# A Strassen-like form with seven products for half of an MLP's down projections

## Chip, core and metric

The kernel runs on one core of one Trainium2 chip. The metric is the device time of one execution in microseconds (us). Before the change three runs took 2326.5, 2327.51 and 2328.44 us, median 2327.51 us.

## The reference

Two decoder layers over 256 tokens of width 2048 in float32: layer 0 with differential attention, layer 1 with a gated linear recurrence. After each of the two stands the same MLP, which this change concerns, and then a gated input embedding (`ple`).

```python
def rmsnorm(x, g):
    y = xf * lax.rsqrt(jnp.mean(xf * xf, axis=-1, keepdims=True) + EPS)
    return (y * g).astype(x.dtype)

def sqrelu_mlp(xn, w_up, w_down):          # w_up (2048, 8192), w_down (8192, 2048)
    return jnp.square(jax.nn.relu(xn @ w_up)) @ w_down

for i in range(2):
    h = h + mixer_i(rmsnorm(h, g_mix[i]))
    h = h + sqrelu_mlp(rmsnorm(h, g_mlp[i]), w_up[i], w_down[i])
    h = h + sigmoid(rmsnorm(h, g_ple[i]) @ w_ple_gate[i]) * (p[i] @ w_ple_proj[i])
```

## The kernel before

**Products in three parts.** Every float32 operand is split into two parts of type float32r, `hi` and `lo`, with `hi + lo` equal to the value. A product of 128 tokens, 128 k and 512 columns is then three matmuls into the same PSUM bank (`mm3`, lines 248 to 251): hi x hi, hi x lo, lo x hi. The weights come as fp32 from HBM and are split on the chip: ScalarE copies (line 255), VectorE subtracts (line 256).

**The weight stream.** `stream` (from line 332) walks over a list of groups. A group is one product over some k-tiles for 512 columns; its weights are cut into chunks of 4 k-tiles x 512 columns (1 MB, one DMA on SyncE's queue, `w_raw`, 3 buffers) and each chunk into two subs of 2 k-tiles (`w_hi` and `w_lo`, 4 buffers each: the slots). While sub j is multiplied, the loop issues loads two chunks ahead and splits three subs ahead (`W_SPLIT - 1`). The tile framework places all waits. It also orders each engine's instructions by a plan made at compile time, in which the order of the code is the priority, and gives a tile a free buffer of its pool.

**The MLP.** `mlp` (from line 628) works on 1024 of the 8192 hidden columns at a time. Two *up* groups give the hidden values transposed (`flip`: the weights stand in the array, the normed tokens, hi and lo side by side, move), each with 16 k-tiles x 4 blocks x 2 matmuls (line 391; 512 and 256 columns) into four banks. Its eviction (lines 644 to 646) adds the halves of each bank (ScalarE copy, VectorE add), does relu and square in one VectorE operation and splits the result into two tiles of the tag `big` (4 buffers of 8 KiB a partition). Four *down* groups follow, one for each 512 output columns, with 8 k-tiles: 2 token tiles x 8 k x 3 = 48 matmuls into two banks, after which line 589 adds each bank, scaled, to the residual `h`. The order is up(0), up(1), down(0), up(2), down(1) and so on, in units of 1024 columns, so down works on values evicted a stage ago. The last down groups feed the next norm: squares on ScalarE (line 302), transposes on TensorE through the two banks `tp` (line 317), scaled splits (lines 259 and 260).

PSUM has eight banks: six of the tag `acc` and two `tp`.

Of the kernel before, what the change touches and what calls it, by code (L numbers as in the profile page):

```python
# [17 lines left out]
P = 128  # L18
# [11 lines left out]
KC = 4  # L30
# [12 lines left out]
class Chunk:  # L43
    """Up to KC k-tiles of one weight column block, moved by one DMA."""

# [5 lines left out]
class Sub:  # L51
    """SK k-tiles of a chunk, split into two float32r parts."""

    own = None

# [4 lines left out]
class Group:  # L60
    """One product over nk k-tiles: [256 tokens, 512 columns], or its transpose where flip is set."""

    def __init__(self, w, k0, nk, n0, lhs, evict, flip=False):
        self.lhs, self.evict, self.nk, self.flip, self.subs, self.pre = lhs, evict, nk, flip, [], {}
        for c in range(0, nk, KC):
            n = min(KC, nk - c)
            r0 = (k0 + c) * P
            src = w[r0 : r0 + n * P, n0 : n0 + NB].rearrange("(c p) n -> p c n", p=P)
            ch = Chunk(src, n)
            self.subs += [Sub(ch, s) for s in range(0, n, SK)]  # L70


@with_exitstack
def trunk_kernel(ctx: ExitStack, tc, a, out):
# [35 lines left out]

# [1 line left out]
    state = {"tick": 0}  # L112
# [13 lines left out]

# [1 line left out]
    h = cp.tile([P, NT, D], F32, name="h")  # L128
# [117 lines left out]

# [1 line left out]
    def mm3(ps, lh, ll, rh, rl, start, stop):  # L248
# [34 lines left out]
    class Wide(Operand):  # L283
        """Both parts of a k-tile side by side: one [k, 512] moving operand."""

# [44 lines left out]

# [1 line left out]
    def stream(groups):  # L332
        subs = [s for g in groups for s in g.subs]
        chunks = []
        for s in subs:
            if not chunks or chunks[-1] is not s.chunk:
                chunks.append(s.chunk)
        cidx = {id(c): i for i, c in enumerate(chunks)}
        done = {"load": 0, "split": 0}

        def load_to(i):
            while done["load"] < min(i + 1, len(chunks)):
                c = chunks[done["load"]]
                c.raw = wraw.tile([P, KC, NB], F32, name="w_raw")
                if c.pre is not None:
# [6 lines left out]
                done["load"] += 1  # L352

        def split_to(i):
            while done["split"] < min(i + 1, len(subs)):
# [4 lines left out]
                else:  # L360
                    s.hi = wsp.tile([P, SK, NB], F32R, name="w_hi")
                    s.lo = wsp.tile([P, SK, NB], F32R, name="w_lo")
                    split(s.hi, s.lo, s.chunk.raw[:, s.k0 : s.k0 + SK])
                done["split"] += 1

        j = 0
        for g in groups:
            acc = [psum([P, NB]) for _ in range(4 if g.flip else NT)]
            kt = 0
            for i, s in enumerate(g.subs):  # L370
# [5 lines left out]
                if s.own is not None:  # L376
                    continue
                if g.flip:
                    x = g.lhs()
# [27 lines left out]

# [1 line left out]
    pT = {}  # L409
# [14 lines left out]

# [1 line left out]
    n0 = Norm(G_MIX)  # L426
# [197 lines left out]

# [1 line left out]
    FC = 1024  # L626
    NFC = DFF // FC
    FKT = FC // P

    def mlp(l, norm_in, norm_out):  # L630
        hid = {}

        def up_evict(c, half):
            """relu(.) ** 2 of a transposed product; the row factor squared goes onto the next product"""

            def evict(acc):
                if half == 0:
                    hid[c] = Operand(big([P, FKT, SEQ], F32R), big([P, FKT, SEQ], F32R))
                for b in range(2):
                    u = t2([P, 2, SEQ])  # L640
                    for i in range(2):
                        ps = acc[2 * b + i]
                        other = t1([P, SEQ])
                        nc.scalar.copy(other, ps[:, SEQ:])  # L644
                        nc.vector.tensor_tensor(u[:, i], ps[:, :SEQ], other, op=ALU.add)
                    nc.vector.scalar_tensor_tensor(u, in0=u, scalar=0.0, in1=u, op0=ALU.max, op1=ALU.mult)
                    ks = slice(half * 4 + 2 * b, half * 4 + 2 * b + 2)
                    split(hid[c].hi[:, ks], hid[c].lo[:, ks], u)

            return evict  # L650

        def up(c):
            for half in range(2):
                groups.append(
                    Group(a["w_up"][l], 0, KT_D, c * FC + half * NB, norm_in, up_evict(c, half), flip=True)
                )

        def down(c):
            for nb in range(4):
                groups.append(  # L660
                    Group(
                        a["w_down"][l], c * FKT, FKT, nb * NB, lambda kt, t, c=c: hid[c].lhs(kt, t),
                        residual_evict(nb, norm_out if c == NFC - 1 else None, lambda: norm_in().r2),
                    )
                )

        up(0)
        for c in range(1, NFC):
            up(c)
            down(c - 1)  # L670
        down(NFC - 1)

# [1 line left out]
    def ple(l, norm_in, norm_out):  # L674
# [49 lines left out]

# [1 line left out]
    w_in = a["w_in_rec"][0]  # L726
# [183 lines left out]

    # the first group takes x as it comes
    first = groups[0]
# [64 lines left out]
```

## Time and profile before

| | |
|---|---|
| median of three runs | 2327.51 us (2326.5 to 2328.44) |
| profiled execution, span | 2326.8 us |
| TensorE (PE) busy | 2308.8 us, 11467 matmuls |
| VectorE (DVE) busy | 1424.6 us |
| ScalarE (ACT) busy | 1193.6 us |
| DMA queue of the weights (q1) | 436.24 MB, 57.3% of 16 engines' span |

The page gives no time of the profiled execution other than its span, which lies among the runs. Times are microseconds unless marked ns. The busy time of PE is modelled and overlaps from one matmul to the next; how fast matmuls follow each other is seen in the start times.

### The profile page before, as it was taken

The numbers are of one execution on the slowest core, as the hardware profiler recorded it, in microseconds if no ns is written. First come the engines' busy times: TensorE is split into PE (matmuls) and PEld (weight loads), VectorE is DVE, ScalarE is ACT, GpSimd is POOL, SyncE is SP. The second block draws the span as 40 slices with busy tenths as digits, with TensorE's granted clock in tenths as the row PEclk, the third lists the DMA queues.
The fourth block names the chain that finished last, engine by engine and source line by source line (L and its number), as shares of the span: only waits on it lengthen the run. The fifth ranks groups of instructions, "written<-read, shape, count | busy, mean of one in ns | idle before, by whom it ended". The sixth has DMA issues, their size and how long they took to land.

```text
span 2326.8 us, 28564 instructions
## 1 busy us (share of the span) xinstructions
PE 2308.8 (99%) x11467; PEld 1946.9 (84%) x11467; DVE 1424.6 (61%) x1704; ACT 1193.6 (51%) x1594; POOL 44.7 (2%) x79
## 2 busy tenths in 40 slices
PE   8999999999999999999999999999999999999999
PEld 6888888888888888888888887888888888888887
DVE  6676655565565665566566767566565555565654
ACT  6555554444444444444558887454444444444453
POOL 2100000000000000000000000000000000000000
PEclk9999999999999999999999999999999999999999
DMA  7454555555565655655566565556565565555554
GB/s 241 163 185 163 165 179 181 185 195 189 191 197 184 198 188 192 196 185 181 189 193 219 187 212 181 181 182 198 184 197 190 191 197 184 198 189 191 177 199 148
DMA packets 225396, 438.95 MB, mean 189 GB/s; under 512 B 7582, under 2 KB 16416, under 8 KB 225264
## 3 DMA queue, kind: packets, MB, share of 16 engines
q1 hardware_dynamic: 224608, 436.24, 57.3%
q8 instruction: 89, 1.46, 0.3%
q0 software_dynamic: 608, 0.89, 0.2%
q14 instruction: 43, 0.35, 0.0%
q10 hardware_dynamic: 48, 0.02, 0.0%
HBM read 435.01 MB, written 2.10 MB: 188 GB/s over the span
## 4 chain that ended last, share of the span: by engine, by line
PE 94%; DVE 2%; ACT 2%; DMA 1%; issue 1%; SPq 0%; POOL 0%; DVEq 0%; ACTq 0%
PE acc L391 31%; PE acc L251 21%; PE acc L249 20%; PE acc L250 20%; PE tp L317 1%; DVE w_lo L256 1%; ACT w_hi L255 1%; DMA w_raw<-in_w_gate_x_dram 0%; DVE t L770 0%; DMA h<-in_x_dram 0%; PE tp L458 0%; DVE big L827 0%; ACT L810 0%; SPq L351 0%; ACT L788 0%
## 5 line engine op out<-in xcount | busy, mean ns | idle before, releaser
L256 DVE TENSOR_TENSOR w_lo<-w_raw,w_hi 128x1024 fp32r<-128x1024 f32 x808 | 987.4, 1224 | 781.4 <-ACT w_hi L255 779.9
L255 ACT CAST w_hi<-w_raw 128x1024 fp32r<-128x1024 f32 x808 | 849.0, 1052 | 979.8 <-PE acc L251 605.7
L391 PE MATMUL acc<-x,w_hi 128*128 128x512 f32 x2048 | 704.8, 394 | 0.0
L391 PE MATMUL acc<-x,w_lo 128*128 128x256 f32 x2048 | 547.8, 278 | 0.0
L249 PE MATMUL acc<-w_hi,x 128*128 128x512 f32 x1152 | 457.1, 397 | 0.0
L250 PE MATMUL acc<-w_lo,x 128*128 128x512 f32 x1152 | 450.2, 391 | 1.9 <-DVE w_lo L256 1.8
L251 PE MATMUL acc<-w_hi,x 128*128 128x512 f32 x1152 | 450.5, 391 | 0.0
L391 PEld LDWEIGHTS acc<-x,w_hi 128*128 128x128 f32 x2048 | 376.0, 188 | 78.6
L249 PE MATMUL acc<-w_hi,big 128*128 128x512 f32 x1024 | 399.7, 390 | 0.0
L251 PE MATMUL acc<-w_hi,big 128*128 128x512 f32 x1024 | 398.6, 389 | 0.0
L250 PE MATMUL acc<-w_lo,big 128*128 128x512 f32 x1024 | 398.4, 389 | 0.0
L391 PEld LDWEIGHTS acc<-x,w_lo 128*128 128x128 f32 x2048 | 384.7, 188 | 11.2
L251 PEld LDWEIGHTS acc<-w_hi,x 128*128 128x128 f32 x1152 | 216.8, 188 | 46.8 <-DVE x L256 0.2
L250 PEld LDWEIGHTS acc<-w_lo,x 128*128 128x128 f32 x1152 | 217.2, 189 | 45.0 <-DVE w_lo L256 3.0
L249 PEld LDWEIGHTS acc<-w_hi,x 128*128 128x128 f32 x1152 | 216.8, 188 | 41.7
L251 PEld LDWEIGHTS acc<-w_hi,big 128*128 128x128 f32 x1024 | 192.2, 188 | 40.3
L250 PEld LDWEIGHTS acc<-w_lo,big 128*128 128x128 f32 x1024 | 192.3, 188 | 39.8
L249 PEld LDWEIGHTS acc<-w_hi,big 128*128 128x128 f32 x1024 | 192.2, 188 | 39.0
L589 DVE SCALAR_TENSOR_TENSOR h<-acc,n_r,h 128x512 f32<-128x512 f32 x128 | 89.9, 744 | 0.0
L644 ACT COPY t<-acc 128x256 f32<-128x256 f32 x128 | 47.5, 371 | 22.8 <-PE acc L391 20.6
L259 ACT ACTIVATE x<-tp,cols_a 128x256 fp32r<-128x256 f32 (+1 forms) x72 | 35.7, 496 | 39.5 <-DVE x L260 39.5
L260 DVE SCALAR_TENSOR_TENSOR x<-tp,cols_a,x 128x256 fp32r<-128x256 f32 (+1 forms) x72 | 36.8, 511 | 18.8 <-ACT x L259 18.8
(173 smaller groups left out, 1064.2 us busy)
## 6 DMA issues: line engine op xcount, KB each, us to landing
w_raw<-in_w_up_dram SPq DMA_DIRECT2D x128, 1024.0 KB, 5.2
w_raw<-in_w_down_dram SPq DMA_DIRECT2D x128, 1024.0 KB, 5.1
w_raw<-in_w_qkv_dram SPq DMA_DIRECT2D x47, 1024.0 KB, 5.2
w_raw<-in_w_ple_gate_dram SPq DMA_DIRECT2D x32, 1024.0 KB, 5.2
w_raw<-in_w_in_rec_dram SPq DMA_DIRECT2D x32, 1024.0 KB, 5.5
w_raw<-in_w_o_attn_dram SPq DMA_DIRECT2D x16, 1024.0 KB, 5.2
w_raw<-in_w_o_rec_dram SPq DMA_DIRECT2D x16, 1024.0 KB, 5.1
w_raw<-in_w_ple_proj_dram SPq DMA_DIRECT2D x8, 512.0 KB, 3.7
```

Of the source, the lines that this page charges most:

```text
L249: nc.tensor.matmul(ps, lhsT=lh, rhs=rh, start=start, stop=False)
L250: nc.tensor.matmul(ps, lhsT=lh, rhs=rl, start=False, stop=False)
L251: nc.tensor.matmul(ps, lhsT=ll, rhs=rh, start=False, stop=stop)
L255: nc.scalar.copy(hi, src)
L256: nc.vector.tensor_tensor(lo, src, hi.bitcast(F32), op=ALU.subtract)
L259: nc.scalar.activation(hi, src, AF.Copy, scale=scale)
L260: nc.vector.scalar_tensor_tensor(lo, in0=src, scalar=scale, in1=hi.bitcast(F32), op0=ALU.mult, op1=ALU.subtract)
L317: nc.tensor.transpose(tp[:, i, t * P : (t + 1) * P], h[:, t, (k0 + i) * P : (k0 + i + 1) * P], ident)
L391: nc.tensor.matmul(o, lhsT=lh, rhs=rh, start=k == 0 and n == 0, stop=k == g.nk - 1 and n == 1)
L589: nc.vector.scalar_tensor_tensor(hb, in0=acc[t], scalar=scale()[:, t : t + 1], in1=hb, op0=ALU.mult, op1=ALU.add)
L644: nc.scalar.copy(other, ps[:, SEQ:])
```

## The change

The hidden columns are taken in 16 batches of 4 k-tiles (512 columns) a layer. Every second batch, with an even number, is multiplied in a *seven* form: for each pair of k-tiles the two token tiles and two k-tiles are a 2 x 2 matrix of blocks X, two k-tiles and two column blocks of 512 a matrix W, and the 2 x 2 product is formed from seven block products of sums of blocks in place of eight. The up eviction makes the sums S1 to S4 of X and splits them along with X; the sums of W (U1, T2, T3, T4) are made on VectorE from the raw chunks and split like weights. Seven partial sums P1 to P7 lie in seven PSUM banks and the plain batches' one left (Z) in the eighth, P3 and Z in the two `tp` banks.

A down group now covers 1024 output columns (one half) and mostly four batches: seven, plain, seven, plain. Its order: up(0), up(1), down(half 1; 0, 1), up(2), up(3), down(half 0; 0 to 3), up(4), up(5), down(half 1; 2 to 5), ..., up(14), up(15), down(half 0; 12 to 15), down(half 1; 14, 15). That is nine down groups a layer where there were 32. `middle` combines P1, P5, P6, P7 in SBUF after their last use, `evict` adds eight parts to `h`.

In the MLPs (`ring = 1`) raw chunks get a fourth buffer (of the tag `big`) and split weights two more slots (of `v4` and `big`), six in all. The relu and the square move from one VectorE operation to two of ScalarE. The rest of the diff drops comments and docstrings.

```diff
+S3, S1, S2, S4, X11, X12, X22, X21 = range(8)
+FORMS = (
+    ("W11", X11, "P1"), ("U1", S1, "P5"), ("T2", S2, "P6"), ("T3", S3, "P7"), ("W21", X12, "P2"),
+    ("T4", X22, "P4"), ("W22", S4, "P3"),
+)
+SUMS = {"U1": ("W11", "W12"), "T2": ("U1", "W22"), "T4": ("T2", "W21"), "T3": ("W12", "W22")}
+BT = 4
...
+class SevenGroup:
+    def products(self, i, s):
+        b, form, nj = self.what[i]
+        x, out = self.hid[b], []
+        if nj is None:
+            _, f, k = FORMS[form]
+            for j in range(2):
+                out.append((k,) + x.form(j, f) + (s.hi[:, j], s.lo[:, j]))
+        else:
+            n, j = nj
+            for t in range(NT):
+                for kk in range(SK):
+                    out.append((self.plain(n)[t],) + x.lhs(2 * j + kk, t) + (s.hi[:, kk], s.lo[:, kk]))
...
         def load_to(i):
-                c.raw = wraw.tile([P, KC, NB], F32, name="w_raw")
+                turn["raw"] += c.ring
+                if c.ring and turn["raw"] % (W_RAW + 1) == 0:
+                    c.raw = big([P, KC, NB])
+                else:
+                    c.raw = wraw.tile([P, KC, NB], F32, name="w_raw")
...
+        def split_form(s):
+            bl = s.blocks
+            src = bl.of(FORMS[s.form][0])
+            nc.scalar.copy(s.hi, src)
+            after = FORMS[s.form + 1][0] if s.form + 1 < len(FORMS) else None
+            if after in SUMS:
+                load_to(cidx[id(bl.chunks[1])])
+                one, two = (bl.of(nm) for nm in SUMS[after])
+                bl.sums[after] = t4([P, SK, NB])
+                nc.vector.tensor_tensor(bl.sums[after], one, two, op=ALU.add)
+            nc.vector.tensor_tensor(s.lo, src, s.hi.bitcast(F32), op=ALU.subtract)
...
         def split_to(i):
-                    s.hi = wsp.tile([P, SK, NB], F32R, name="w_hi")
-                    s.lo = wsp.tile([P, SK, NB], F32R, name="w_lo")
-                    split(s.hi, s.lo, s.chunk.raw[:, s.k0 : s.k0 + SK])
+                    turn["split"] += s.chunk.ring
+                    at = turn["split"] % (W_SPLIT + 2) if s.chunk.ring else 2
+                    if at == 0:
+                        s.hi, s.lo = (v4([P, SK, NB], F32R) for _ in range(2))
+                    elif at == 1:
+                        both = big([P, 2, SK, NB], F32R)
+                        s.hi, s.lo = both[:, 0], both[:, 1]
+                    else:
+                        s.hi = wsp.tile([P, SK, NB], F32R, name="w_hi")
+                        s.lo = wsp.tile([P, SK, NB], F32R, name="w_lo")
+                    if s.blocks is None:
+                        split(s.hi, s.lo, s.chunk.raw[:, s.k0 : s.k0 + SK])
+                    else:
+                        split_form(s)
...
+                if seven:
+                    prods = g.products(i, s)
+                    for q in prods:
+                        if q[0] not in acc:
+                            acc[q[0]] = ps_tp.tile([P, NB], F32, name="tp") if q[0] in ("P3", "Z") else psum([P, NB])
+                    for k, lh, ll, rh, rl, first, last in prods:
+                        nc.tensor.matmul(acc[k], lhsT=lh, rhs=rh, start=first, stop=False)
+                        nc.tensor.matmul(acc[k], lhsT=ll, rhs=rh, start=False, stop=False)
+                    for k, lh, ll, rh, rl, first, last in prods:
+                        nc.tensor.matmul(acc[k], lhsT=lh, rhs=rl, start=False, stop=last)
+                    if i == g.mid:
+                        g.middle(acc)
...
         def up_evict(b):
+                hid[b] = bt = batch(b)
+                for j in range(2):
+                    f = t4([P, 8, P]) if bt.seven else t2([P, 4, P])
...
+                        nc.vector.tensor_tensor(halves[i], two(ps[:, :SEQ]), two(other), op=ALU.add)
-                    nc.vector.scalar_tensor_tensor(u, in0=u, scalar=0.0, in1=u, op0=ALU.max, op1=ALU.mult)
+                    nc.scalar.activation(x, x, AF.Relu)
+                    nc.scalar.activation(x, x, AF.Square)
+                    if bt.seven:
+                        nc.vector.tensor_tensor(
+                            f[:, S3 : S1 + 1], f[:, X11 : X22 + 1 : X22 - X11],
+                            f[:, X21 : X21 + 1].broadcast_to([P, 2, P]), op=ALU.subtract,
+                        )
+                        nc.vector.tensor_tensor(f[:, S2], f[:, S1], f[:, X11], op=ALU.add)
+                        nc.vector.tensor_tensor(f[:, S4], f[:, X12], f[:, S2], op=ALU.subtract)
+                    split(bt.hi[:, j], bt.lo[:, j], f[:, :X21] if bt.seven else f)
...
+            def middle(acc):
+                c1, cb = t4([P, 2, NB]), t4([P, 2, NB])
+                keep["P1"], keep["M"], keep["B"], keep["N"] = c1[:, 0], c1[:, 1], cb[:, 0], cb[:, 1]
+                nc.scalar.copy(keep["P1"], acc["P1"])
+                nc.vector.tensor_tensor(keep["M"], keep["P1"], acc["P6"], op=ALU.subtract)
+                nc.vector.tensor_tensor(keep["B"], acc["P7"], keep["M"], op=ALU.add)
+                for k, o in (("M", "M"), ("N", "B")):
+                    nc.vector.scalar_tensor_tensor(
+                        keep[k], in0=acc["P5"], scalar=-1.0, in1=keep[o], op0=ALU.mult, op1=ALU.subtract
                     )
+            def evict(acc):
+                r2 = norm_in().r2
+                for t, n, ps, other in ((0, 0, "P2", "P1"), (1, 0, "P4", "B"), (0, 1, "P3", "M"), (1, 1, "Z", "N")):
+                    hb = h[:, t, hs[n]]
+                    for part in (acc[ps], keep[other]):
+                        nc.vector.scalar_tensor_tensor(
+                            hb, in0=part, scalar=r2[:, t : t + 1], in1=hb, op0=ALU.mult, op1=ALU.add
+                        )
+                if bs[-1] == NBT - 1:
+                    for n in range(2):
+                        norm_out().feed(2 * half + n)
...
+        for b in range(0, NBT, 2):
+            up(b)
+            up(b + 1)
+            down(int(b % 4 == 0), range(max(b - 2, 0), b + 2))
+        down(1, range(NBT - 2, NBT))
```

## Rows read from the trace of the kernel before

**Rows 1.** The page: span, busy time by engine, chain that ended last.

```profile
span 2326.8 us, 28564 instructions
...
PE 2308.8 (99%) x11467; PEld 1946.9 (84%) x11467; DVE 1424.6 (61%) x1704; ACT 1193.6 (51%) x1594; POOL 44.7 (2%) x79
...
PE 94%; DVE 2%; ACT 2%; DMA 1%; issue 1%; SPq 0%; POOL 0%; DVEq 0%; ACTq 0%
```

**Rows 2.** Costliest groups: line engine op, tiles, shapes, count | busy us, mean ns | idle before.

```profile
L255 ACT CAST w_hi<-w_raw 128x1024 fp32r<-128x1024 f32 x808 | 849.0, 1052 | 979.8 <-PE acc L251 605.7 <-PE acc L391 350.8 <-issue 11.6
...
L256 DVE TENSOR_TENSOR w_lo<-w_raw,w_hi 128x1024 fp32r<-128x1024 f32 x808 | 987.4, 1224 | 781.4 <-ACT w_hi L255 779.9
...
L391 PE MATMUL acc<-x,w_hi 128*128 128x512 f32 x2048 | 704.8, 394 | 0.0
...
L251 PE MATMUL acc<-w_hi,big 128*128 128x512 f32 x1024 | 398.6, 389 | 0.0
...
L589 DVE SCALAR_TENSOR_TENSOR h<-acc,n_r,h 128x512 f32<-128x512 f32 x128 | 89.9, 744 | 0.0
```

**Rows 3.** Chain in order of time: start us, length us, engine, tile, line.

```profile
537.50 44.40 PE acc L391 x256
...
845.89 0.23 PE acc L250
846.12 0.23 PE acc L251
```

**Rows 4.** Windows, layer 0: two up groups, four down groups, a whole period.

```profile
core 0: us, PE busy (x) PEld busy (x) DVE busy (x) ACT busy (x) POOL busy (x), PEclk, DMA share, GB/s
537.50:581.90 44.40, 44.40 (x258) 38.80 (x257) 24.63 (x28) 20.28 (x25) 0.00 (x0) 1.00 0.59 192
581.90:625.40 43.50, 43.50 (x193) 36.01 (x193) 27.14 (x30) 18.29 (x19) 0.00 (x0) 1.00 0.58 192
889.18:977.10 87.92, 87.92 (x450) 74.85 (x449) 51.79 (x57) 38.56 (x44) 0.00 (x0) 1.00 0.59 192
```

**Rows 5.** Groups by shape: smaller VectorE and ScalarE operations.

```profile
L644 ACT COPY t<-acc 128x256 f32<-128x256 f32 x128 | 47.5, 371 | 22.8 <-PE acc L391 20.6
...
L645 DVE TENSOR_TENSOR t<-acc,t 128x256 f32<-128x256 f32 x128 | 47.9, 416 | 0.0
...
L646 DVE SCALAR_TENSOR_TENSOR t<-t 128x512 f32<-128x512 f32 x64 | 43.6, 682 | 0.0
...
L256 DVE TENSOR_TENSOR big<-t,big 128x512 fp32r<-128x512 f32 x64 | 43.8, 684 | 0.0
...
L255 ACT CAST big<-t 128x512 fp32r<-128x512 f32 x64 | 39.7, 620 | 0.8
...
L302 ACT ACTIVATE t<-h 128x512 f32<-128x512 f32 x48 | 29.8, 623 | 0.0
...
L792 DVE TENSOR_TENSOR big<-t,t 128x256 f32<-128x256 f32 x16 | 6.8, 423 | 15.7 <-ACT t L790 15.7
...
L260 DVE SCALAR_TENSOR_TENSOR x<-tp,cols_a,x 128x256 fp32r<-128x256 f32 x64 | 30.8, 481 | 18.8 <-ACT x L259 18.8
```

**Rows 6.** Waits of SP's DMA queue (us, times, longest); down loads (KB, us to landing).

```profile
SPq L351 <- DVE w_lo L256: 1846.0, 364, 10.0
...
w_raw<-in_w_down_dram SPq DMA_DIRECT2D x128, 1024.0 KB, 5.1
```

**Rows 7.** ScalarE in order of time where up gives way to down.

```profile
845.97 1.05 ACT L255 CAST w_hi<-w_raw 128x1024 fp32r<-128x1024 f32 x1
846.91 0.62 ACT L255 CAST big<-t 128x512 fp32r<-128x512 f32 x1
```

**Rows 8.** Windows of the recurrence in layer 1 with VectorE or ScalarE busiest.

```profile
1300.00:1340.00 40.00, 37.78 (x186) 31.05 (x185) 36.10 (x51) 32.45 (x47) 0.00 (x0) 1.00 0.67 212
1390.00:1440.00 50.00, 48.43 (x232) 40.00 (x231) 37.69 (x47) 43.45 (x60) 0.00 (x0) 1.00 0.49 156
```

**Rows 9.** Groups: table loads.

```profile
L810 ACT ACT_TABLE_LOAD x11 | 14.1, 1283 | 0.2
```

More of the change, by code (lines that the diff above doesn't have):

```diff
@@ L43 @@
 class Chunk:
+    ring = 0
     def __init__(self, src, nk):
@@ L51 @@
 class Sub:
-    own = None
+    own, blocks, form = None, None, None
     def __init__(self, chunk, k0):
@@ new lines, with __init__, of, plain @@
+class Blocks:
+    def __init__(self, w, b, n0):
+        r0 = b * BT * P
+        rows = w[r0 : r0 + BT * P].rearrange("(c p) n -> p c n", p=P)
+        self.chunks = [Chunk(rows[:, :, n0 + i * NB : n0 + (i + 1) * NB], BT) for i in range(2)]
+        for c in self.chunks:
+            c.ring = 1
+        self.sums = {}
+    def of(self, name):
+        if name in self.sums:
+            return self.sums[name]
+        return self.chunks[int(name[2]) - 1].raw[:, int(name[1]) - 1 :: 2]
+class SevenGroup:
+    flip = False
+    def __init__(self, w, batches, n0, hid, middle, evict):
+        self.hid, self.middle, self.evict, self.subs, self.pre = hid, middle, evict, [], {}
+        self.what = []
+        for b, seven in batches:
+            bl = Blocks(w, b, n0)
+            if seven:
+                for i, (form, _, _) in enumerate(FORMS):
+                    s = Sub(bl.chunks[0 if form in ("W11", "W21") else 1], 0)
+                    s.blocks, s.form = bl, i
+                    self.subs.append(s)
+                    self.what.append((b, i, None))
+            else:
+                for n in range(2):
+                    for j in range(BT // SK):
+                        self.subs.append(Sub(bl.chunks[n], j * SK))
+                        self.what.append((b, None, (n, j)))
+        self.first, self.last = {}, {}
+        for i, (_, form, nj) in enumerate(self.what):
+            for k in [FORMS[form][2]] if nj is None else self.plain(nj[0]):
+                self.first.setdefault(k, i)
+                self.last[k] = i
+        self.mid = max(self.last[k] for k in ("P1", "P5", "P6", "P7"))
+    @staticmethod
+    def plain(n):
+        return (("P2", "P4"), ("P3", "Z"))[n]
+    def products(self, i, s):
[10 more added lines that the diff above has]
+                    out.append((self.plain(n)[t],) + x.lhs(2 * j + kk, t) + (s.hi[:, kk], s.lo[:, kk]))
+        res = []
+        for n, o in enumerate(out):
+            k = o[0]
+            same = [m for m, q in enumerate(out) if q[0] == k]
+            res.append(o + (self.first[k] == i and n == same[0], self.last[k] == i and n == same[-1]))
+        return res
@@ L335, in stream @@
         for s in subs:
-            if not chunks or chunks[-1] is not s.chunk:
+            if not any(c is s.chunk for c in chunks[-2:]):
                 chunks.append(s.chunk)
@@ L339, in stream @@
         done = {"load": 0, "split": 0}
+        turn = {"raw": 0, "split": 0}
         def load_to(i):
@@ L367, in stream @@
         for g in groups:
-            acc = [psum([P, NB]) for _ in range(4 if g.flip else NT)]
+            seven = isinstance(g, SevenGroup)
+            if seven:
+                acc = {}
+            else:
+                acc = [psum([P, NB]) for _ in range(4 if g.flip else NT)]
             kt = 0
@@ L623, in trunk_kernel, with is_seven, batch, up_evict @@
         groups.append(Group(a["w_o_attn"][0], 0, KT_D, nb * NB, lambda kt, t: oT().lhs(kt, t), residual_evict(nb, n_mlp0)))
-    FC = 1024
-    NFC = DFF // FC
-    FKT = FC // P
+    NBT = DFF // (BT * P)
+    SLOTS = 4
+    def is_seven(b):
+        return b % 2 == 0
     def mlp(l, norm_in, norm_out):
-        hid = {}
-        def up_evict(c, half):
-            def evict(acc):
[L637 to L640, printed above, removed]
+        hid, space = {}, {}
+        def batch(b):
+            if not is_seven(b):
+                both = big([P, 2, 2, 4, P], F32R)
+                return Batch(False, both[:, 0], both[:, 1])
+            if "x" not in space:
+                space["x"] = x32([P, 2, 2, 2, 7, P])
+            both = space["x"][:, b % SLOTS // 2]
+            return Batch(True, both[:, 0], both[:, 1])
+        def up_evict(b):
+            def evict(acc):
+                hid[b] = bt = batch(b)
+                for j in range(2):
+                    f = t4([P, 8, P]) if bt.seven else t2([P, 4, P])
+                    x = f[:, X11:] if bt.seven else f
+                    halves = (x[:, 0 : X21 - X11 + 1 : X21 - X11], x[:, X12 - X11 : X22 - X11 + 1])
@@ L641, in evict @@
                     for i in range(2):
-                        ps = acc[2 * b + i]
+                        ps = acc[2 * j + i]
                         other = t1([P, SEQ])
                         nc.scalar.copy(other, ps[:, SEQ:])
-                        nc.vector.tensor_tensor(u[:, i], ps[:, :SEQ], other, op=ALU.add)
-                    nc.vector.scalar_tensor_tensor(u, in0=u, scalar=0.0, in1=u, op0=ALU.max, op1=ALU.mult)
-                    ks = slice(half * 4 + 2 * b, half * 4 + 2 * b + 2)
@@ L667, in mlp @@
[L667 to L671, printed above, removed]
+                        two = lambda v: v.rearrange("p (t c) -> p t c", t=2)
+                        nc.vector.tensor_tensor(halves[i], two(ps[:, :SEQ]), two(other), op=ALU.add)
[8 more added lines that the diff above has]
+                        nc.vector.tensor_tensor(f[:, S4], f[:, X12], f[:, S2], op=ALU.subtract)
@@ new lines, in evict, with up, down @@
+                    split(bt.hi[:, j], bt.lo[:, j], f[:, :X21] if bt.seven else f)
+            return evict
+        def up(b):
+            g = Group(a["w_up"][l], 0, KT_D, b * NB, norm_in, up_evict(b), flip=True)
+            for s in g.subs:
+                s.chunk.ring = 1
+            groups.append(g)
+        def down(half, bs):
+            n0 = half * 2 * NB
+            hs = [slice(n0 + i * NB, n0 + (i + 1) * NB) for i in range(2)]
+            keep = {}
+            def middle(acc):
[7 more added lines that the diff above has]
+                        keep[k], in0=acc["P5"], scalar=-1.0, in1=keep[o], op0=ALU.mult, op1=ALU.subtract
+                    )
+            def evict(acc):
[7 more added lines that the diff above has]
+                if bs[-1] == NBT - 1:
+                    for n in range(2):
+                        norm_out().feed(2 * half + n)
+            groups.append(SevenGroup(a["w_down"][l], [(b, is_seven(b)) for b in bs], n0, hid, middle, evict))
```

25 lines of the change are left out of this document (11 added, 14 removed).

## The prediction

> **What bounds the kernel now.** First the page's busy shares: TensorE (PE) is busy 99% of 2326.8 us, VectorE (DVE) 61%, ScalarE (ACT) 51% [rows 1]. The chain that ended last says the same: 94% PE, two lines of DVE and ACT at 2% each [rows 1]. The span lies 0.7 us under the median of the three runs, 2327.51; I work with the span and add 0.7 at the end. Then the costliest groups: the down projections' 3072 products (three lines of 1024 with `big` as weights), the up projections' 2048 pairs, and 808 weight splits, 1.05 us on ACT and 1.22 us on DVE each [rows 2]. A matmul's own duration (389 ns) is not its pace, since they overlap; the chain in the third view gives the pace. A down product comes every 0.227 us, and two up groups stand as one unbroken piece of 44.40 us [rows 3]. The windows confirm it: 44.40 us of up and 43.5 us of down, PE busy for all of it, DVE for 24.6 and 27.1, DMA engines at 0.58 [rows 4]. One period of the MLP (two up groups, four down groups) is 87.92 us; 192 products in 43.52 us are 0.2267 us each. So the MLPs are bound by PE alone, with no stall to win back, and only fewer products can shorten them.
>
> What runs beside PE is paced by it: ACT's splits waited 350.8 and 605.7 us for PE to free a split buffer [rows 2], and the DVE behind them for ACT. The splits are thus limited by the four slots, not by DVE or ACT. That matters below.
>
> **The change part by part.**
>
> *Products removed.* A plain batch (4 k-tiles, two column blocks) takes 2 x 4 x 2 x 3 = 48 products; a batch in seven forms 7 x 2 x 3 = 42, of the same shape, 512 columns, with one weight load each as before. Each layer has 8 such batches, each for two column halves: 32 in all, 192 products fewer. At 0.2267 us [rows 3, 4] that is 43.5 us. Nothing suggests another pace for them. A period becomes 44.4 + 180 x 0.2267 = 85.2 us. Up projections and DMA bytes stay: each weight is still loaded once, 1 MB per chunk.
>
> *DVE added in down.* A plain batch needs 4 splits per half, a seven batch 7 and 4 sums. The trace has no sum of two weight blocks; it is a 128x1024 fp32 tensor_tensor like the split, so 1.22 us [rows 2], and not less than 0.94 (the pace of ACT's pass over as many elements, 845.97 to 846.91 [rows 7]) nor more than two of 0.68 [rows 5]. A seven batch then costs DVE 11 x 1.224 = 13.5 us against 42 x 0.2267 = 9.5 us of PE, a plain one 4.9 against 10.9. After form T3 of the group's last seven batch come the sums of products (`middle`): two of 0.68 and two of 0.74, 2.9 us; at the end of a group (`evict`) 4 x 0.74 + 4 x 0.68 = 5.7 us [rows 2, 5]. Before, the same h update took 8 x 0.74 per four groups.
>
> *Up eviction.* DVE loses the relu-square (0.68 each) and, for seven batches, gains a subtraction of 256 columns (0.42), two operations of 128 (0.29 by the step from 512 to 256) and a split of 896 in place of 512 (1.09, between 0.68 and 1.22). That makes 4 x 0.416 + 2 x 2.1 = 5.9 us for a seven batch and 3.0 for a plain one, 4.4 before. ACT gains relu and square, 0.62 each by its copies of that size [rows 5].
>
> *Sum by engine over one period* of two ups and a down group of four batches: DVE 16 x 1.224 (splits of up) + 8.9 (up evictions) + 8 x 1.224 + 22 x 1.224 (two plain, two seven batches) + 2.9 + 5.7 = 73.8 us of 85.2 (87%; 51.8 of 87.92 before [rows 4]); ACT 38 splits x 1.05, 8 copies x 0.37, 8 passes of relu and square x 0.62, 3.1 for the parts hi and 0.6 in `middle`, 51.7 us (61%). PE stays the longest. But in the down group alone DVE needs 45.3 us while PE needs 40.8. So it depends on work done ahead.
>
> *Work ahead.* Count from PE's end of the up groups. With six slots form n may be split when PE has left the sub six before it: forms 0 to 4 at -13.9, -11.1, -8.3, -5.6, -2.8 (up subs last 2.78 us). So 5 forms and their sums, up to 5 + 4 operations or 11 us of DVE, fit into the up group, where DVE is idle 45% [rows 4]. At 0 remain the up eviction and forms 5 and 6. The eviction is a chain over two engines: copy 0.37, add 0.42, relu, square, hi 0.62 each on ACT, lo 0.68, for two halves; I get its ACT part done at 4.3, so hi of form 5 at 5.3, lo at 6.6. PE wants that lo at 5 x 1.36 + 0.9 = 7.7. Cover left: 1.1 us. After that the plain batch (10.9 us of PE for 4.9 of DVE) lets DVE refill all slots, the second seven batch starts with up to 5 forms ready, `middle` has 15 us before its group ends, and the final `evict` (5.7 us) stands before up subs of 2.78 us with up to 5 ready. I cost all of this at 0 per period. A raw buffer: chunk pairs are held until form 6 is split, so the next pair lands about 13 us into the group (5.1 us each [rows 6]); it is needed by PE at 20.4. Also 0. SP's queue holds only these loads in the MLPs and waited for DVE's splits all along [rows 6].
>
> *Where cover is missing.* The last two groups of each layer follow each other without up groups between, and the first feeds the next norm. After its end DVE has 5.7 us of `evict`, then 8 scaled splits of 0.48, and forms 4 to 6 of the next batch (3.7 and a sum), all before PE has run 9.5 us; the transposes also need the two `tp` banks, which now hold P3 and Z. The work is about 14 us for 9.5, with some done before: a stall of 1.5 to 7, I take 4, twice. The feed after the last group now comes as one lump of 5.7 us before the gate's k-tiles 8 to 15 instead of 1.4 us before 12 to 15; PE has 13.6 us of other products meanwhile. I take 1, twice (0 to 4).
>
> Sum: 2326.8 - 43.5 + 8 + 2 = 2293.3, with 0.7 on top **2294**. The least is all of it hidden, 2284.
>
> **The rivals.**
>
> *A, the gain is lost (2334).* The engines' queues keep the order of the code, in which splits are only three subs ahead, and the up eviction stands in front of form 3. Then hi of form 3 comes at 5.3 where PE wants it at 4.1, and each of forms 4 to 6 keeps part of the delay: I add up 2.5 us for each of the 16 groups that follow an up eviction, 40 us on the forecast: 2334. For it: the lookahead count in the loop is unchanged at W_SPLIT - 1, and the eviction is longer by ACT's passes. Against it: in the trace a weight split at 845.97 went ahead of the eviction's own split at 846.91 though it is issued later [rows 7], so the order is not that of the code.
>
> *B, slower.* DVE becomes the bound in the down groups: 45.3 against 40.8 in 14 groups of four batches, 26.9 against 20.4 in 4 groups of two: 63 + 26 = 89 us of stall, 2373 if nothing is done ahead. The point of decision is 43.5 / 18 = 2.4 us of stall a group. For it: the recurrence's stretch with DVE at 90% lost 2.2 of 40 us of PE, and one with ACT at 87% 1.6 of 50 [rows 8]; 4% of the two MLPs' 1364 us would be 55, 2338. Against it: those stretches have PE waiting for chains through table loads and scans, while here weights depend on nothing but slots. I price it at 2350.
>
> *C, half of it.* The margin of 1.1 us at form 5 is missed by 1 to 2 us in each of these 16 groups, since every step of the chain is engine to engine: 2294 + 24 = 2318.
>
> *D, table loads.* A table load took 1.28 us [rows 9]. Were Relu in another table than the rest, 64 halves x 2 loads would put 164 us on ACT and some 5 us into each of the 16 tight places: about 2370. Square and Copy run side by side without a load [rows 5, 9]; Relu does not occur in this trace. The Trainium skill ("ScalarE: Activation LUTs", Table sets) says relu is in every set, which no row here shows.
>
> *E, the up evictions come onto the path.* ACT's passes over 512 columns took 0.62 us, and the DVE relu-square 0.68 in one pass [rows 5], so the move makes the chain 2 x 0.62 - 0.68 = 0.56 us longer per half. If PE waited for each of the 64 halves, that would be 36 us: 2330. Against it: no product needs a batch sooner than 9.5 us after its eviction. The Trainium skill ("ScalarE: Activation LUTs", Rules for kernel authors) tells to use VectorE, not ScalarE, for relu; the rows of this kernel bear it out as to the length of the pass, not as to what waits for it.
>
> **How the numbers follow.** Forecast 0.60 (own range 2283 to 2306), C 0.16, A 0.07, B 0.11, D 0.02, E 0.04. 0.2%, about 5 us, is what a measurement can tell from no change. The range runs from the least, 2284, less the 2 us by which the runs of before differ, to 2320, past C; beyond lie A, B, D, E and a little of C. Faster take the forecast, C and the lower ends of A and E: 0.78; within 0.2% the middle of A and E: 0.06; slower B, D and the upper ends of A and E: 0.16.
>
> **What would show it.** PE instructions fewer by 192 and a pace of 0.227 us inside a seven batch; a period of 85.2 us without PE waits, DVE near 87% in it; stalls only where two down groups meet (1 to 7 us) and at the gate's start. Wrong if PE waits for `w_lo` or `w_hi` in forms 3 to 6 of a group's first batch (A, C), in all seven batches (B), or if ACT shows table loads in the up eviction (D).

## The result, and the profile after

Four runs of the changed kernel took 2303.47 to 2304.05 us, median 2303.72; four of the kernel before beside them had a median of 2327.11. The ratio is 0.990, 95% interval 0.9885 to 0.9913: faster by 23 us. The forecast was 2294; the time lies within the range, 10 us above the forecast. The profiled execution took 2303.79 us with a span of 2301.9, so 1.9 us lie around the span where I had added 0.7.

The page of the changed kernel, to be held against [rows 1]: 192 products fewer, VectorE (DVE) busy 285 us longer, ScalarE (ACT) 162 us.

```profile
span 2301.9 us, 29004 instructions
...
PE 2277.8 (99%) x11275; PEld 1913.4 (83%) x11275; DVE 1709.6 (74%) x2048; ACT 1355.5 (59%) x1836; POOL 47.3 (2%) x79
```

PE is still "99% busy", yet the span shrank by 24.9 us and not by the 43.5 of the products. The windows show where to look: three periods, then each MLP from its first up product to the first product of the gate behind it. The second fence is one such window of the kernel before.

```profile
1827.21:1912.99 85.78, 85.78 (x437) 72.76 (x437) 68.13 (x77) 47.48 (x59) 0.00 (x0) 1.00 0.59 203
1912.99:1999.00 86.01, 86.01 (x437) 72.88 (x437) 69.24 (x77) 50.59 (x61) 0.00 (x0) 1.00 0.56 189
1739.58:1827.21 87.63, 86.30 (x438) 72.77 (x437) 69.56 (x77) 48.00 (x59) 0.00 (x0) 1.00 0.56 193
...
402.40:1098.40 696.00, 691.61 (x3513) 584.89 (x3513) 556.41 (x627) 396.48 (x495) 1.08 (x3) 1.00 0.56 191
...
1501.50:2197.40 695.90, 691.61 (x3514) 584.62 (x3513) 557.86 (x627) 395.68 (x496) 2.52 (x3) 1.00 0.55 190
```

```profile
403.70:1111.30 707.60, 707.60 (x3617) 602.26 (x3616) 421.31 (x466) 320.06 (x384) 1.08 (x3) 1.00 0.58 191
```

The period was 87.92 us [rows 4] and was to become 85.2. It repeats as 85.78, 86.01 and 87.63. In the first two PE is busy for every microsecond and still takes 0.6 and 0.8 too long: here products come slower. In the third it stands still for 1.3. The granted clock is 1.00 throughout, so the clock is not the reason.

The chain in order of time shows both. Under [rows 3] two up groups were one piece of 44.40 us; now, with the same 256 products, they are 44.70 to 44.99:

```profile
1769.81 14.67 PE acc L537 x83
1784.88 0.95 ACT w_hi L464
1785.83 1.04 ACT t L807 x2
1786.88 1.04 ACT t L808 x2
1788.32 0.62 ACT big L356
1788.94 0.96 ACT big L464
1789.94 0.51 PE acc L518
...
1827.21 44.70 PE acc L537 x256
...
1912.99 44.99 PE acc L537 x256
...
1999.00 44.90 PE acc L537 x256
...
2172.00 2.08 DVE h L848 x3
2174.10 0.68 ACT t L403 x2
2175.09 0.71 ACT t L403 x2
...
2176.16 0.94 ACT v L464
2177.14 0.50 PE acc L518
```

The top is the stall of the 87.63 period: the up groups end at 1784.48, ACT splits a form (L464), then runs the relu and the square of the up eviction (L807, L808) and the split of its result (L356, tag `big`), and only then the split of form 3 into the slot of tag `big`, for which PE waits. The bottom is the place where the last two down groups meet: `evict` on DVE, squares, then the split that PE waits for. Waits of PE in the down groups, total us, times, longest:

```profile
PE acc L518 <- ACT big L464: 5.3, 4, 1.3
...
PE acc L518 <- ACT w_hi L464: 1.3, 1, 1.3
PE acc L518 <- ACT v L464: 1.1, 1, 1.1
```

Four waits for `big` are two in each MLP. The slower pace shows in the start times of one form whose split weights lie in the slot of tag `v4` (shown as `v`): eight steps in 1.86 to 1.87 us, 0.233 us each, where a down product took 0.2267 on average by [rows 4].

```profile
1798.23 0.39 PE L518 MATMUL acc<-v,big 128*128 128x512 f32 x1
1798.46 0.39 PE L519 MATMUL acc<-v,big 128*128 128x512 f32 x1
...
1799.86 0.39 PE L519 MATMUL acc<-v,big 128*128 128x512 f32 x1
1800.09 0.63 PE L521 MATMUL acc<-v,big 128*128 128x512 f32 x2
```

To size the parts I charged each product of an MLP with the time from its start to the next start, and called a stall what goes beyond 0.2267 us in a step of over 0.44. A pair is the two products that the up groups take for one block and one k-tile:

| us in one MLP | before | after (layer 0, 1) |
|---|---|---|
| up, 1024 pairs | 355.75 | 359.07, 358.76 |
| down, 1536 or 1440 products | 349.03 | 329.51, 329.69 |
| stalls | 0.0 | 5.04, 5.14 |
| transposes of the next norm | 2.83 | 2.35, 2.28 |
| sum | 707.6 | 696.0, 695.9 |

In experiment 6, where the old pace is back, the 1440 products take 327.1. So in both MLPs together: 43.9 removed, 6.3 lost to the pace of up, 5.0 to the pace of down, 10.2 to stalls, 1.0 won back in the transposes and 1.5 outside the MLPs: 24.9, the difference of the spans.

### The profile page after: what moved, and what is told of

It reads as the page before. It is cut to its first block, busy times and chain, and to the rows that moved or that the text cites. A ratio compares the mean times of both kernels' runs of the same rounds, so it can differ in the third digit from the quotient of the medians.

```text
span 2301.9 us, 29004 instructions
## 1 busy us (share of the span) xinstructions
PE 2277.8 (99%) x11275; PEld 1913.4 (83%) x11275; DVE 1709.6 (74%) x2048; ACT 1355.5 (59%) x1836; POOL 47.3 (2%) x79
## 3 DMA queue, kind: packets, MB, share of 16 engines
q1 hardware_dynamic: 220256, 432.04, 55.5%
## 5 line engine op out<-in xcount | busy, mean ns | idle before, releaser
L357 DVE TENSOR_TENSOR w_lo<-w_raw,w_hi 128x1024 fp32r<-128x1024 f32 x465 | 564.2, 1221 | 304.5 <-ACT w_hi L356 304.4
L356 ACT CAST w_hi<-w_raw 128x1024 fp32r<-128x1024 f32 x465 | 486.6, 1051 | 419.4 <-PE acc L352 214.9
L537 PE MATMUL acc<-x,w_hi 128*128 128x512 f32 x1368 | 477.3, 396 | 0.0
L537 PE MATMUL acc<-x,w_lo 128*128 128x256 f32 x1368 | 368.5, 279 | 0.0
L537 PEld LDWEIGHTS acc<-x,w_hi 128*128 128x128 f32 x1368 | 251.9, 188 | 54.7
L537 PEld LDWEIGHTS acc<-x,w_lo 128*128 128x128 f32 x1368 | 257.8, 188 | 7.4
L464 ACT CAST w_hi<-t 128x1024 fp32r<-128x1024 f32 x85 | 89.2, 1051 | 128.8 <-PE acc L537 73.9
L537 PE MATMUL acc<-x,big 128*128 128x512 f32 (+1 forms) x688 | 127.7, 338 | 0.0
L356 ACT CAST w_hi<-big 128x1024 fp32r<-128x1024 f32 x87 | 90.7, 1050 | 62.6 <-PE acc L537 26.7
L537 PE MATMUL acc<-x,v 128*128 128x512 f32 (+1 forms) x672 | 124.8, 338 | 0.0
L537 PEld LDWEIGHTS acc<-x,big 128*128 128x128 f32 x688 | 107.9, 188 | 15.5
L537 PEld LDWEIGHTS acc<-x,v 128*128 128x128 f32 x672 | 105.9, 188 | 15.0
L471 DVE TENSOR_TENSOR w_lo<-w_raw,w_hi 128x1024 fp32r<-128x1024 f32 x64 | 78.0, 1219 | 31.9 <-ACT w_hi L464 31.9
```

Of the source, the lines that this page charges most:

```text
L357: nc.vector.tensor_tensor(lo, src, hi.bitcast(F32), op=ALU.subtract)
L464: nc.scalar.copy(s.hi, src)
L471: nc.vector.tensor_tensor(s.lo, src, s.hi.bitcast(F32), op=ALU.subtract)
L537: nc.tensor.matmul(o, lhsT=lh, rhs=rh, start=k == 0 and n == 0, stop=k == g.nk - 1 and n == 1)
```

## Experiments

Times are medians, with the ratio to the kernel before and its interval. "Up" is an MLP's up part as in the table.

**1. Is it the start of the `v4` tiles?** One of the two new split slots is the pair of `v4` tiles, which the attention used before as values. In the compiled program they begin at byte 218080 of a partition; the four old split slots, the tokens and `big` all begin 32 bytes past a multiple of 256 (61216, 93984, 162592). First the start was moved by 192 bytes:

```diff
+XW = SEQ + 8
...
-            xt = t4([P, 4, SEQ + 3])
+            xt = t4([P, 4, XW])
...
```

> The changed kernel with one size altered: the t4 buffers are 4224 instead of 4160 bytes, so that the v4 tiles, which serve as one of the six split slots, begin 32 bytes above a multiple of 128 like all other split slots (in the changed kernel: 96 above). Theory 1 (place): the products that read their weights from v4 are slow (233.3 ns against 226.7 ns) because of where the tile begins, and the slow spells of the up groups (2.83 us a sub in place of 2.77) start there. Then v4 products run at 226.7 ns, the up groups fall from 359 to about 356 us a layer, and the whole is 7 to 11 us faster than the changed kernel: about 2294. Theory 2 (activity): the pace falls because VectorE and ScalarE work more beside it and the slots only look different; then nothing changes, 2304. The three stalls of 1.5 us a layer stay in both.

Measured: 2301.69 (0.9888, 0.9874 to 0.9903), up 357.6 and 357.3; the products from `v4` now step by 229, 237 or 238 ns for the most part, in place of 233. So the place has an effect, but this was not a good place. Then all tiles were moved by 96 bytes as well, `v4` to 218368:

```diff
+    cp.tile([P, 24], F32, name="pad")
     ident = cp.tile([P, P], F32, name="ident")
```

> The same, and 96 bytes of padding ahead of all other tiles, so that every weight, operand and split tile begins at a multiple of 128 bytes instead of 32 above one. Theory 1 in its strong form: it is the distance to a 128-byte line that counts, and 32 above costs something as well, for all products: 512 columns would then take less than 226.7 ns, by up to 7 ns (the step between 226.7 and 233.3), and the whole would fall by up to 11000 x 6.6 ns = 70 us, to about 2230. In its weak form only unequal places of the two operands cost: then the result is that of the run before, about 2294. Theory 2: 2304.

2301.39 (0.9886, 0.9871 to 0.9901), up 357.5 and 357.1, and the down products of the other slots kept their 226.7. Both `v4` and the others now begin elsewhere, at the same distance from each other as in the run above, and up stays within 0.3 us: this speaks for the distance and against the start of each tile by itself.

**2. Is it the slot at all, without the change?** The kernel before with a fifth split slot of `v4` in its MLPs, and nothing else:

```diff
...
-                    s.hi = wsp.tile([P, SK, NB], F32R, name="w_hi")
-                    s.lo = wsp.tile([P, SK, NB], F32R, name="w_lo")
+                    turn["split"] += s.ring
+                    if s.ring and turn["split"] % (W_SPLIT + 1) == 0:
+                        s.hi, s.lo = (v4([P, SK, NB], F32R) for _ in range(2))
+                    else:
+                        s.hi = wsp.tile([P, SK, NB], F32R, name="w_hi")
+                        s.lo = wsp.tile([P, SK, NB], F32R, name="w_lo")
...
```

> The kernel before, with one part of the change alone: in the MLPs a fifth split slot made of the two v4 tiles, which begin 96 bytes above a multiple of 128. It has no work to win, since no product waited for a split. Theory 1 (place): a fifth of the down products, some 307 a layer, takes 233.3 instead of 226.7 ns (2 us a layer) and the up groups have slow spells (3 us a layer): 2327 + 10 = about 2337. Theory 2 (activity): VectorE and ScalarE do the same work as before, so no change: 2327.

2339.32 (1.0048, 1.0031 to 1.0065): 11 us slower, up 359.5 and 359.3, products from `v4` at 233 ns. Its chain has the long up pieces of the changed kernel:

```profile
1744.09 44.90 PE acc L397 x256
1832.81 44.98 PE acc L397 x256
1921.69 44.93 PE acc L397 x256
```

**3. Is the stall at form 3 one of order?** Splits five subs ahead in the MLPs, not three, so that form 3 is issued ahead of the up eviction:

```diff
-                split_to(j + W_SPLIT - 1)
+                split_to(j + (W_SPLIT + 1 if s.chunk.ring else W_SPLIT - 1))
```

> The changed kernel, but in the MLPs the loop issues splits five subs ahead instead of three, so that the first five forms of a down group stand ahead of the up eviction in the order of the code. Theory (buffers given out in the order of the code): form 3 of every third down group waits for its buffer of the tag big behind the plain batch's own buffer of that tag, which is taken by the eviction; with five ahead it no longer does, and the two stalls of 1.5 us in each MLP go: 2304 - 6 = about 2298. Rival (the eviction's ScalarE passes themselves hold form 3 back): the stalls stay, 2304. Second rival: early splits push the eviction back, PSUM banks come free later and PE stalls elsewhere: 2304 or more.

2295.58 (0.9862, 0.9847 to 0.9877), 8 us below the changed kernel. ScalarE in order of time: the split into `big` now comes 11 us ahead of relu and square, and no such wait is left. Stalls are 1.5 and 1.3 us an MLP; up stays at 359.1 and 358.8. So the order of issue explains the stalls at form 3, and with them 1.4 us at the meeting of the last two groups, and not the pace.

```profile
1770.47 1.05 ACT L464 CAST big<-t 128x1024 fp32r<-128x1024 f32 x1
...
1781.90 1.15 ACT L807 ACTIVATE t<-t 128x512 f32<-128x512 f32 x2
```

**4. Fewer slots.** Five, without `v4`, splits four ahead; and four, without `v4` and `big`, three ahead:

```diff
-                    at = turn["split"] % (W_SPLIT + 2) if s.chunk.ring else 2
-                    if at == 0:
-                        s.hi, s.lo = (v4([P, SK, NB], F32R) for _ in range(2))
-                    elif at == 1:
+                    at = turn["split"] % (W_SPLIT + 1) if s.chunk.ring else 2
+                    if at == 1:
...
-                split_to(j + W_SPLIT - 1)
+                split_to(j + (W_SPLIT if s.chunk.ring else W_SPLIT - 1))
```

> The changed kernel without the split slot of the two v4 tiles (five slots: four and the one of the tag big), with splits issued four subs ahead. Theory (the v4 slot sets the pace): without it no product runs at 233.3 ns, the up groups stay in the fast pace (about 356 us a layer in place of 359) and down products at 227.2 ns on average: 4.5 us a layer, 9 us in all, better than the run with five subs ahead (2295.6): about 2287, if five slots are enough; stalls at forms 3 to 6 of a down group would show that they are not, 1 to 3 us for each of 16 groups, up to 2320. Rival (the pace has to do with the seven form or with busier VectorE and ScalarE): up groups stay at 359 us a layer and the time at 2296 or above.

```diff
-                    at = turn["split"] % (W_SPLIT + 2) if s.chunk.ring else 2
+                    at = 2
```

> The changed kernel with four split slots as before the change (the fourth raw buffer stays). Theory of the prediction (work ahead makes the seven form free): with three forms ready at the start of a down group, forms 3 to 6 come behind the up eviction and cost about 2.5 us in each of 16 groups, and the place where two down groups meet loses more: 2304 + 40 + 5, less 9 for the pace that the extra slots cost: about 2340. Rival: the lookahead is worth nothing, since the loop issues only three subs ahead anyway: 2304 - 9 = 2295.

Five slots: 2291.22 (0.9843, 0.9829 to 0.9858), up 355.75 in both layers, stalls of 2.9 and 5.5 us where the last two groups meet. Four slots: 2295.47 (0.9861, 0.9845 to 0.9878), up 355.75, small waits that lengthen its down products by 3 us an MLP (330.3) and 1.8 us of stalls. I had expected 2340 of four slots; the rival's 2295 came out, though not its reason, that lookahead is worth nothing: the small waits show that it covered some of the work. The change was 8 us faster without its two new slots than with them: as placed and as ordered, they cost more in pace and in stalls at form 3 than they bring in cover.

**5. The eviction's passes.** Relu and square in one VectorE operation again (one run):

```diff
-                    nc.scalar.activation(x, x, AF.Relu)
-                    nc.scalar.activation(x, x, AF.Square)
+                    nc.vector.scalar_tensor_tensor(x, in0=x, scalar=0.0, in1=x, op0=ALU.max, op1=ALU.mult)
```

> The changed kernel with relu and square in one VectorE operation as before, in place of two on ScalarE. Theory (rival E is wrong, up evictions lie beside PE): only the two stalls of 1.5 us a layer shorten, since form 3's split gets ScalarE about 2 us sooner: 2298 to 2304. If E were right in part, 10 us or more would go: 2294 or less. If VectorE's load were what counts (0.68 us more for each of 64 halves): slower than 2304.

2297.12, 6.6 us below the changed kernel; PE no longer waits for `big`, and up is 359.1 and 358.8. With ACT's two passes gone form 3 comes in time: the same stall, mended from its other end.

**6. Place first.** As 3, and the `v4` tiles get their place ahead of others (byte 159520), by a small write at the start:

```diff
+    for _ in range(2):
+        nc.gpsimd.memset(v4([P, 8]), 0.0)
     rows_g = t1([P, P])
...
```

> The run with five subs ahead and six slots (2295.6), with only the place of the tags in memory altered: the v4 tiles come first in their pool (byte 159520 of a partition in place of 218080), all other tags of the pool move up by 8192 bytes. If the pace of the v4 products comes from where these tiles lie in memory, it changes: up groups 356 to 359 us a layer, v4 products other than 233.3 ns, and at best 2287. If it comes from the slot being two tiles of a tag that others use too, and not from its place, nothing changes: 2296.

2285.74 (0.9819, 0.9804 to 0.9834): 18 us below the changed kernel. Up is 355.75 in both layers, products from `v4` come every 226.7 ns (eight in 1.81 us in the second fence), and its up pieces are 44.40 us long and 85.20 apart:

```profile
1644.53 44.40 PE acc L539 x256
1729.73 44.40 PE acc L539 x256
1814.93 44.40 PE acc L539 x256
```

```profile
1786.21 0.39 PE L520 MATMUL acc<-v,big 128*128 128x512 f32 x1
...
1788.02 0.84 PE L523 MATMUL acc<-v,big 128*128 128x512 f32 x3
```

**7. Which rule of place?** In 6 the tiles are lower in memory and also a multiple of 256 bytes from the other operands. Two paddings in front of `v4` in the version of 3 keep them behind all other tiles and change only the distance (64 bytes: 208 floats become 16):

```diff
...
+            if hp == 0:
+                nc.gpsimd.memset(wk.tile([P, 208], F32, tag="pad", name="pad", bufs=1), 0.0)
```

> ahead5 with 832 bytes a partition of padding in front of the two v4 tiles, which now begin at byte 218912 of a partition, still behind all other tiles. Theory of distance: the pace depends on the distance from the v4 tile to the other operand tiles (tokens hi at 93984, split slots from 61216) modulo 1024; it was 192 in ahead5 and 0 in v4_first, and is 0 here. Then the v4 products come every 226.7 ns, the up groups of an MLP take 355.8 us and the run about 2286. Rival, place: what is far up in memory is slow; then up 359 and 2296, as ahead5.

> ahead5 with 64 bytes a partition of padding in front of the v4 tiles (byte 218144): their distance to the other operand tiles is 256 modulo 1024. Distance modulo 1024 or 512: slow products of about 233 ns, up 358 to 359 us, 2294 to 2297. Distance modulo 256 or less: 226.7 ns, up 355.8, 2286. Place (far up is slow): 2296.

832 bytes: 2285.70 (0.9818, 0.9803 to 0.9833). 64 bytes: 2285.24 (0.9816, 0.9802 to 0.9831). Both have up at 355.75 and 226.7 ns from `v4`. So 64 bytes of padding are worth 10 us beside experiment 3. Height in memory is refuted, and so is a modulus of 512 or 1024. Up pieces of the 64-byte version:

```profile
1729.28 44.40 PE acc L537 x256
1814.48 44.40 PE acc L537 x256
```

| start of `v4` | distance to the other operands, modulo 256 | step of its products, ns | up, us |
|---|---|---|---|
| 218080 (after, 2, 3, 5) | 192 | 233 | 358.8 to 359.5 |
| 218272, 218368 (1) | 128 | 224 to 238, mixed | 357.1 to 357.6 |
| 159520, 218144, 218912 (6, 7) | 0 | 226.7 | 355.75 |

**8. The slot in the kernel before, well placed.** 2 with the edit of 6:

> The kernel before with a fifth split slot of v4 tiles, as before_v4 (2339), but v4 tiles given their place first, 0 modulo 1024 from the other operand tiles. Distance or place: the slot costs nothing and gains nothing, 2326 to 2328, products 226.7 ns in both up and down. Rival, a fifth slot is itself harmful (other tags, other semaphores): about 2339 again.

2327.20 (0.9998, 0.9989 to 1.0008), up 355.75. What 2 lost was place alone; a fifth slot by itself neither costs nor gains there.

**9. The eviction again, with both causes gone.** 6 with the edit of 5:

> v4_first with relu and square in one VectorE operation again. relu_dve took away the 3 us of stall an MLP at form 3, but v4_first has none left there. If the eviction only mattered for the big slot: the same as v4_first, 2285 to 2287. If the two ScalarE passes still hold something up (the stalls of 1.3 to 1.5 us an MLP where two down groups meet are on VectorE's side, so more VectorE work could also lengthen them): 2282 or 2289.

2285.73 (0.9819, 0.9804 to 0.9834), the same as 6. Once form 3 is split ahead, it made no difference here which engine does relu and square.

## Why the prediction was right, and where it missed

**Products removed: right.** 192 products went, and at the pace of [rows 3, 4] they are worth the 43.5 us of the sum. In the version of experiment 6 the period is 85.20 us, the predicted figure. The bytes did not quite stay: the queue of the weights moved 432.04 MB, not 436.24, since the new list of chunks loads the recurrence's gate weights (`w_gate_a`, `w_gate_x`) 8 times each and not 16. That lies outside the MLPs, where all differences together are 1.5 us.

**"Nothing suggests another pace" was the step that failed**, and with it "up projections stay": +11.3 us against 0. I had taken the pace of a product as given by its shape. It also depends on the place of the slot. The diff showed that two slots of other tags come in; the trace before could not show their pace, as its MLPs never multiply from `v4`, and I gave the step no upper bound. But that trace did show that the shape alone does not give the pace: the second up group of each MLP took 22.59 us, the third and those behind it 22.20, PE busy throughout and the granted clock 1.00. Layer 0, second and third group of the kernel before, columns as in [rows 4]:

```profile
426.83:449.42 22.59, 22.59 (x129) 19.60 (x128) 13.50 (x18) 10.81 (x14) 0.00 (x0) 1.00 0.59 190
449.42:471.62 22.20, 22.20 (x130) 19.41 (x128) 13.43 (x18) 10.82 (x14) 0.00 (x0) 1.00 0.58 186
```

This slow group stands unchanged in experiments 4 and 6 to 9, so a badly placed slot is not the only thing that brings the slower pace.

**The range held by its width.** It had been drawn past C, whose waits did not come, and a pace that the prediction had not considered took that room. The 9.7 us above the forecast are the 11.3 of pace and 1.2 around the span, less smaller terms.

**Stalls: the sum right by luck, the places wrong.** 10 us were predicted (8 at the meeting of the last two groups, 2 at the gate) and 10.2 measured, but 4.2 at the meeting, none at the gate and 6.0 at form 3, which I had at 0. There rival A's mechanism holds in part. In the code form 3 takes its `big` buffer after the batch that the eviction writes, and its split is issued after it; forms 4 and 5, issued later still but into `w_hi`, were split before it (1781.74 and 1784.77 in the fence below, form 3 at 1788.84). That the shared tag is what holds the order is my reading of this; the run of experiment 3 shows that an earlier issue removes the wait. From [rows 7] I had concluded that the order is not that of the code; that row shows a split into `w_hi`, whose slots are not shared with the eviction. A period issues 38 subs, two more than a multiple of six, so only every third period has the `big` slot at form 3: 4 stalls of 1.5 us, not 16 of 2.5.

**Work ahead, margin at form 5: wider than predicted.** The up groups ended at 1784.48. Form 5's hi part was expected 5.3 us later, behind the eviction; even in a stalled period it began at 1784.77, ahead of relu and square, and form 6's at 1789.79. PE did not wait for forms 4 to 6 (C wrong). ScalarE from form 4 on:

```profile
1781.74 1.05 ACT L464 CAST w_hi<-w_raw 128x1024 fp32r<-128x1024 f32 x1 [4.89 <-PE acc L537]
...
1784.77 1.06 ACT L464 CAST w_hi<-t 128x1024 fp32r<-128x1024 f32 x1
1785.72 1.15 ACT L807 ACTIVATE t<-t 128x512 f32<-128x512 f32 x2
1786.78 1.14 ACT L808 ACTIVATE t<-t 128x512 f32<-128x512 f32 x2
1787.82 1.12 ACT L356 CAST big<-t 128x512 fp32r<-128x512 f32 x2
1788.84 1.04 ACT L464 CAST big<-t 128x1024 fp32r<-128x1024 f32 x1
1789.79 1.05 ACT L464 CAST w_hi<-w_raw 128x1024 fp32r<-128x1024 f32 x1
```

**B wrong; DVE's load over-estimated.** 73.8 us a period were predicted, 68.1 to 69.6 measured (79 to 81%). The durations were right: the sum of weights takes 1.22, as assumed, the split of 896 columns 1.08. In the three period windows of the changed kernel the durations add up to 73.1 to 74.1. But operations on one engine overlap a little, so their sum is more than the busy time; [rows 7] had shown it on ScalarE, where a pass of 1.05 was followed 0.94 after its start. Two sums in a row on VectorE in experiment 6 start 1.13 us apart:

```profile
2158.01 1.22 DVE L472 TENSOR_TENSOR t<-t,w_raw 128x1024 f32<-128x1024 f32 x1
2159.14 1.22 DVE L472 TENSOR_TENSOR t<-w_raw 128x1024 f32<-128x1024 f32 x1
```

**D wrong, and E in the main.** E's two passes on ScalarE did lie on the path, but only through form 3: 6.6 us in experiment 5, not 36. Groups by shape of the changed kernel: relu and square at 0.63 and 0.62 us, as the 0.62 of [rows 5]; the table loads of [rows 9] are still 11, none at the eviction.

```profile
L470 DVE TENSOR_TENSOR t<-t,w_raw 128x1024 f32<-128x1024 f32 x64 | 78.0, 1219 | 0.8
...
L807 ACT ACTIVATE t<-t 128x512 f32<-128x512 f32 x64 | 37.9, 629 | 0.3 <-DVE t L806 0.3
L808 ACT ACTIVATE t<-t 128x512 f32<-128x512 f32 x64 | 36.8, 619 | 0.1
...
L1000 ACT ACT_TABLE_LOAD x11 | 14.1, 1283 | 0.2
...
L357 DVE TENSOR_TENSOR x<-t,x 128x896 fp32r<-128x896 f32 x32 | 33.5, 1083 | 0.5 <-ACT x L356 0.5
```

The Trainium skill ("ScalarE: Activation LUTs", Table sets) says that relu is in every set, and the trace agrees: 64 relus, no load beside them. The Trainium skill's rule to use VectorE, not ScalarE, for relu ("ScalarE: Activation LUTs", Rules for kernel authors) was worth 6.6 us in experiment 5, where the square moved with it, and nothing in 9: here it paid only where ScalarE's next operation was waited for.

**Still open.** Why the distance between operand tiles bears on the pace is not explained, nor why in up groups one sub from `v4` can slow the subs behind it as well (pairs of 353 in place of 347 ns, by their start times, mostly until the next sub from `v4` or the end of the group), nor what slows the second up group of each MLP in the kernel before. Only distances of 0, 128 and 192 modulo 256 were tried, and the place of the other operand tiles modulo 256 was changed in one run alone, at a distance of 128. The remaining 1.3 to 1.5 us an MLP at the meeting in experiment 6 was not taken away.

## What to carry to other kernels

When a change brings a new buffer into the operands of matmuls, forecast the pace as a term of its own and measure it: hold the start times of products from the new buffer against the old ones, since the engine shows itself fully busy at both paces. A fixed 64-byte shift was worth nearly half as much here as the whole change (10 of 23 us), so try the place before the slot count. When a slot shares its tag with other data, the order of the code can decide who gets the buffer first, and lookahead then has to reach past the other user.

## What the runs showed of the hardware

A float32r product of 512 columns came every 226.7 ns or every 233.3 ns at the same granted clock of 1.00, by where the tile of one operand lies relative to the others in a partition: 0 modulo 256 bytes was fast in three places, 192 slow in four kernels, 128 between in two. One up group in each MLP ran 1.8% slower (22.59 against 22.20 us) with no such tile in use. Operations that follow each other on VectorE started about 0.1 us before the recorded end of the one before, and ScalarE's likewise (two relus of 0.63 in 1.15 us), so a sum of mean durations gave 6 to 8% too much load.
